# LayerNorm gains and biases in two fused VectorE operations ahead of the transposes, in place of a pass on GpSimd

## Chip, cores and metric

One core of one Trainium2 chip runs the whole program. The metric is the device time in microseconds of an execution; three timed runs of the kernel before are given, and their median is the time that the change is compared with.

## What is computed

Two blocks of a transformer of 512 tokens by 1024 features in float32, four layers in all: latent attention (mla), differential attention (diff), a pooling and gated-convolution mixer (even), and a forgetting attention with a conformer convolution (odd). Behind each mixer comes a SwiGLU feed-forward layer (ffn). Each of the eight steps ends in a sum and a LayerNorm:

```python
h = layernorm(alpha * h + mixer(h), ln_mix_g, ln_mix_b)
h = layernorm(alpha * h + swiglu(h), ln_ffn_g, ln_ffn_b)
# layernorm(x, g, b) = (x - mean(x)) * rsqrt(var(x) + 1e-5) * g + b, over the 1024 features
```

## The kernel before

The residual stream stays in on-chip memory as four tiles `res[t]` of 128 tokens (on partitions) by 1024 features. The products run on TensorE; every float32 operand is given as a high and a low part of 12 significant bits, and each product is three matmuls (`mm3`, L371 to L373). So each weight unit of 512 KB is loaded by the queue of SyncE into `wraw`, copied by ScalarE into the high part `whi` (L170) and subtracted by VectorE or GpSimd into the low part `wlo` (L171). ffn forms its first product by seven products of quarters (Winograd's form), for which VectorE adds and subtracts quarters of the features (`XQ`, L759 to L762, L768) and of the weights (L193 to L198).

Seven of the eight LayerNorms go through `class Norm`, token tile after token tile, within `project_out` (the last one is `LastNorm`, untouched here). For tile t the steps are: the sum with the mixer's product, with row sums (`add_res`, L431); the mean (L448); the squares on ScalarE (L452); the root, a small VectorE operation (L387) and a power on GpSimd (L389, result `lnr`); `scale` (L458), one VectorE operation over 128 x 1024; eight transposes on TensorE into two banks of PSUM (`turn`, L399); `apply` (L464 to L473), which multiplies by the gain and adds the bias of each feature, features being on partitions now, as eight operations over 128 x 128, four on ScalarE (L471) and four on VectorE (L473); then the high parts on ScalarE (L485) and the low parts on VectorE (L489) of the features that the next step's products read (`xh`, `xl`). Ahead of an ffn `apply` also writes the quarters `XQ`, and the high and low parts are taken from them; elsewhere it works in place in PSUM.

`scale` leaves `res[t]` without gain and bias. They come in a separate pass, since only the next sum needs them: `affine_one` (L527 to L532) multiplies and adds over 128 x 512, four operations per tile. Behind the norms of mla, diff, even and odd, `ffn` runs the pass for four tiles on GpSimd, queued at its start behind all that GpSimd has; within odd it runs on GpSimd too, one tile per head; within diff and even it runs on VectorE (`affine`).

```python
def affine_one(eng):
    t, g, b = AFFINE.pop(0)
    for c in range(2):
        s = slice(c * S, (c + 1) * S)
        eng.tensor_mul(res[t][:, s], res[t][:, s], g[:, s])
        eng.tensor_add(res[t][:, s], res[t][:, s], b[:, s])
```

Within `project_out` the order of TensorE, VectorE and ScalarE is the order in which the code is written (`by_hand`); elsewhere the framework's scheduler orders instructions by a timeline of its own, and GpSimd's queue always. Each engine works through its queue in order. The gains and biases of the next norm are loaded into one buffer each (`lng`, `lnb`, L419) by GpSimd's queue, as soon as the pass on the last norm has read them; those of mla by SyncE's. In `project_out`, the first projections of the next step run for tokens 0 to 255 of four weight units, with the transposes of tile 3 behind the second of them, and then for tokens 256 to 511.

Of the kernel before, what the change touches and what calls it, by code (L numbers as in the profile page):

```python
# [50 lines left out]
# the norms in their order  # L51
# [34 lines left out]
# the hidden units of a feed-forward layer in the groups that go into the second product together  # L86
# [3 lines left out]
def ffn_order():  # L90
    """("gate", "up" | "win", unit) of the first product and ("down", columns, pair of chunks) of the second, in turns"""
    order, todo = [], deque()
    for k0, k1 in GROUPS:
        every = (k1 - k0) / len(todo) if todo else 0
        at = every
        for j in range(k0, k1):
            order += [("gate", j), ("up", j)] if j < STD else [("win", j)]
            while todo and j - k0 + 1 >= at - 1e-6:
                order.append(todo.popleft())
                at += every  # L100
        todo.extend(("down", c, u) for c in range(2) for u in range(k0 // 2, k1 // 2))
# [31 lines left out]
class Ring:  # L133
    """A pool's tiles of one tag"""
# [8 lines left out]
class Weights:  # L143
    """Units of weights in the order of their use: each is loaded, and split exactly into two
    parts of 12 significant bits, ahead of its use."""
# [28 lines left out]
    def steps(self):  # L174
        """The next unit, step by step"""
# [10 lines left out]
        # the sums of the quarters, over the quarters that are not needed any more  # L186
# [25 lines left out]
    def may(self, n):  # L212
        """whether one of the next n units is still to be seen to"""
# [100 lines left out]
def kernel(ctx: ExitStack, tc: tile.TileContext, a: dict, out: bass.AP):  # L314
# [15 lines left out]
    def bank(use):  # L330
        """a bank of PSUM, in turns of those for the use"""
# [43 lines left out]
    def split(h, l, src, scale=None):  # L375
        """h + l = src * scale, exactly, in two parts of 12 significant bits."""
# [7 lines left out]
    def rsqrt(ssum, n, count, eps, name):  # L384
        """(ssum / count + eps) ** -0.5 on [P, n]"""
# [6 lines left out]
    def turn(t, bank):  # L392
        """Token tile t of the residual stream with the features on partitions, in two banks"""
# [40 lines left out]
    AFFINE = []  # L434

    class Norm:
        """The LayerNorm of the residual stream, of token tile after token tile, in steps for the
        engines' queues to be laid out by hand"""
        count = 0

        def __init__(self, gb, xT, junk):
            self.gb, self.xT, self.junk, self.ln = gb, xT, junk, Norm.count
            self.m, self.r, self.ps = {}, {}, {}
            Norm.count += 1
# [30 lines left out]
        def source(self, t, c):  # L475
            if XQ:
                return XQ[c, t // 2][:, :, t % 2 * P:(t % 2 + 1) * P]
            return self.ps[t][c].rearrange("p (j t) -> p j t", j=4)

        def parts(self, t, c):  # L480
            return (*part_of(self.xT, t, c), self.source(t, c))
# [8 lines left out]

    class LastNorm:
        """The same behind the last sum, to the output"""
# [28 lines left out]
    def affine():  # L521
        """The gains and biases of the last norm for the residual stream, that only the next sum needs"""
        with after_last():
            while AFFINE:
                affine_one(nc.vector)

    def affine_one(eng):  # L527
        t, g, b = AFFINE.pop(0)
        for c in range(2):
            s = slice(c * S, (c + 1) * S)  # L530
            eng.tensor_mul(res[t][:, s], res[t][:, s], g[:, s])
            eng.tensor_add(res[t][:, s], res[t][:, s], b[:, s])  # L532
# [15 lines left out]
    def mark(*name):  # L548
        """a place in the tensor engine's work, that other work can be queued behind"""
# [8 lines left out]
    class Part:  # L558
        """res = (ALPHA *) res + chunks^T @ w for four chunks, in pieces queued behind marks"""
# [17 lines left out]
    def project_out(chunks, key, gb, xT, names, room, first=True, tail=4, pin=None):  # L577
# [3 lines left out]
        norm = LastNorm(gb, room[0]) if xT is None else Norm(gb, xT, lambda: room[0].tile([P, D], BF16, name="junk", tag=room[1], bufs=room[2]))  # L581
        ps = {}
        cols = {t: ((None, 0, S),) for t in range(NT)}
        if nu == 2:
            # all the weights at hand: one token tile after the other
# [11 lines left out]
            if xT is None:  # L597
# [4 lines left out]
                # the last products are done in two parts  # L602
# [48 lines left out]
        with by_hand():  # L651
            # where the tiles turn: behind two tiles' products, where those of tile 1 are short
            wait = 2 if nu == 2 else 1
            for t in range(NT):
# [3 lines left out]
                if t:  # L658
                    norm.scale(t - 1)
                if t == wait == 2:  # L660
                    norm.turn(0)
                    norm.apply(0, 1)
                    norm.apply(0, 0)
                    norm.high(0, 0)
                    norm.high(0, 1)
                if 1 < t and wait == 1:
                    norm.low(t - 2, 0)
                    norm.low(t - 2, 1)
# [3 lines left out]
                if 1 < t and wait == 2:  # L672
                    norm.low(t - 2, 0)
                    norm.low(t - 2, 1)
# [5 lines left out]
                if t >= wait:  # L680
# [1230 lines left out]
```

## Time and profile before

| what | value |
|---|---|
| timed runs | 2359.85, 2362.2, 2364.51 us; median 2362.2 us |
| profiled execution, first to last instruction (its span) | 2351.2 us |
| TensorE (PE) busy | 2264.4 us, 96% of the span |
| VectorE (DVE) busy | 1842.2 us, 78% |
| ScalarE (ACT) busy | 1033.3 us, 44% |
| GpSimd (POOL) busy | 621.4 us, 26% |
| TensorE's granted clock, mean | 0.985 of 2.4 GHz |

Of the profiled execution the span is given and no other time; the median of the timed runs lies 11.0 us above it. A busy share is a mean over stages: TensorE leads everywhere, so the question in each stage is where it stands still and what it waits for. Matmuls overlap in the records (one that takes 0.28 us starts 0.12 us behind the last), so idle time in a row is slightly less than the start that was lost. Engines are named PE, PEld (weight load), DVE, ACT, POOL and SP in the rows; L12 is line 12 of the kernel before.

### The profile page before, as it was taken

The page shows a single profiled execution, that of the slowest core. Times are in us where ns is not written, and L with a number is a line of the kernel's source. Part 1 is how long each engine was busy: PE and PEld are TensorE (multiplying, and loading weights), DVE is VectorE, ACT ScalarE, POOL GpSimd, SP SyncE. Part 2 cuts the span into 40 slices and gives each one's busy share as a digit, 9 for nine tenths or more (in the row PEclk, how much of TensorE's full clock was granted, in tenths as well). Part 3 has the DMA queues.
Part 4 walks back from the last instruction along what each step waited for, and adds up shares of the span by engine and source line. Part 5 has one row for each costly group of instructions (what it writes and reads, how often), then busy time and mean ns, then how long its engine had stood idle before and what let it go on. Part 6 is the DMA issues. An engine that isn't in the chain of part 4 may idle for free. (4 is left out here: it accounts for less than half of the span.)

```text
span 2351.2 us, 35591 instructions
## 1 busy us (share of the span) xinstructions
PE 2264.4 (96%) x14148; PEld 1996.1 (85%) x14148; DVE 1842.2 (78%) x2810; ACT 1033.3 (44%) x1761; POOL 621.4 (26%) x360
## 2 busy tenths in 40 slices
PE   8999899999999999999999989999997999999997
PEld 8878899998888778999988889999886767899996
DVE  5667888886766688888875698888677767989886
ACT  4654444345555453434353344443344655344441
POOL 2103311112321161111210051111236844311112
PEclk9999999999999999999999999999998999999999
DMA  5212333332321123333323233333222112333331
GB/s 176 61 37 72 99 108 108 98 95 85 99 72 63 37 75 114 108 100 99 98 90 95 92 101 104 108 99 108 81 76 73 36 54 81 108 104 105 99 99 63
DMA packets 59367, 210.52 MB, mean 90 GB/s; under 512 B 6624, under 2 KB 6880, under 8 KB 59200
## 3 DMA queue, kind: packets, MB, share of 16 engines
q1 hardware_dynamic: 56304, 198.97, 26.7%
q0 software_dynamic: 2320, 8.23, 1.0%
q8 instruction: 111, 1.82, 0.3%
q10 hardware_dynamic: 576, 1.05, 0.1%
q14 instruction: 56, 0.46, 0.1%
HBM read 206.12 MB, written 2.10 MB: 89 GB/s over the span
## 5 line engine op out<-in xcount | busy, mean ns | idle before, releaser
L170 ACT ACTIVATE whi<-wraw 128x1024 fp32r<-128x1024 f32 (+3 forms) x528 | 519.8, 987 | 830.8 <-DMA wraw<-in_gu_dram 260.9
L171 POOL TENSOR_TENSOR wlo<-wraw,whi 128x1024 fp32r<-128x1024 f32 (+2 forms) x141 | 358.2, 2544 | 1198.5 <-ACT whi L170 991.1
L171 DVE TENSOR_TENSOR wlo<-wraw,whi 128x1024 fp32r<-128x1024 f32 (+3 forms) x387 | 447.9, 1158 | 140.4 <-ACT whi L170 139.1
L372 PE MATMUL acc<-xl,whi 128*128 128x256 f32 (+1 forms) x1712 | 527.1, 308 | 11.1 <-DVE xl L489 11.1
L373 PE MATMUL acc<-xh,wlo 128*128 128x256 f32 (+1 forms) x1712 | 525.4, 307 | 5.8 <-DVE wlo L171 5.8
L371 PE MATMUL acc<-xh,whi 128*128 128x256 f32 (+1 forms) x1712 | 529.7, 309 | 0.0
L372 PEld LDWEIGHTS acc<-xl,whi 128*128 128x128 f32 x1712 | 325.5, 190 | 37.7 <-DVE xl L489 13.5
L371 PE MATMUL acc<-xs,whi 128*128 128x256 f32 x1216 | 342.6, 282 | 13.7 <-ACT sums L790 7.6
L373 PE MATMUL acc<-xs,wlo 128*128 128x256 f32 x1216 | 344.7, 283 | 3.0 <-DVE wlo L171 3.0
L371 PEld LDWEIGHTS acc<-xh,whi 128*128 128x128 f32 x1712 | 325.5, 190 | 24.2 <-issue 0.4
L373 PEld LDWEIGHTS acc<-xh,wlo 128*128 128x128 f32 x1712 | 325.4, 190 | 23.0 <-DVE wlo L171 6.5
L372 PE MATMUL acc<-xql,whi 128*128 128x256 f32 x1216 | 342.6, 282 | 0.0
L371 PEld LDWEIGHTS acc<-xs,whi 128*128 128x128 f32 x1216 | 231.1, 190 | 21.1 <-ACT sums L790 10.6
L372 PEld LDWEIGHTS acc<-xql,whi 128*128 128x128 f32 x1216 | 229.8, 189 | 5.6
L373 PEld LDWEIGHTS acc<-xs,wlo 128*128 128x128 f32 x1216 | 229.9, 189 | 3.8 <-DVE wlo L171 3.8
L371 PE MATMUL tr<-whi,hh 128*128 128x512 f32 (+1 forms) x296 | 118.6, 401 | 0.0
L372 PE MATMUL tr<-wlo,hh 128*128 128x512 f32 (+1 forms) x296 | 117.4, 397 | 0.0
L373 PE MATMUL ps<-whi,hl 128*128 128x512 f32 x288 | 114.1, 396 | 3.0 <-DVE hl L379 3.0
L373 PE MATMUL tr<-whi,hl 128*128 128x512 f32 (+1 forms) x296 | 116.1, 392 | 0.0
L371 PE MATMUL ps<-whi,hh 128*128 128x512 f32 x288 | 113.4, 394 | 0.3 <-ACT hh L378 0.3
L372 PE MATMUL ps<-wlo,hh 128*128 128x512 f32 x288 | 113.2, 393 | 0.0
L194 DVE TENSOR_TENSOR wraw<-wraw 128x512 f32<-128x512 f32 x76 | 109.2, 1437 | 0.1
(360 smaller groups left out, 4379.9 us busy)
## 6 DMA issues: line engine op xcount, KB each, us to landing
wraw<-in_gu_dram SPq DMA_DIRECT2D x176, 512.0 KB, 3.6
wraw<-in_dn_dram SPq DMA_DIRECT2D x88, 512.0 KB, 3.5
wraw<-in_ev_in_dram SPq DMA_DIRECT2D x16, 512.0 KB, 3.4
wraw<-in_mla_o_dram SPq DMA_DIRECT2D x8, 512.0 KB, 3.6
wraw<-in_df_q_dram SPq DMA_DIRECT2D x8, 512.0 KB, 3.6
wraw<-in_df_k_dram SPq DMA_DIRECT2D x8, 512.0 KB, 3.5
wraw<-in_df_v_dram SPq DMA_DIRECT2D x8, 512.0 KB, 3.4
wraw<-in_df_o_dram SPq DMA_DIRECT2D x8, 512.0 KB, 3.5
```

The costliest lines, as they stand in the source:

```text
L170: self.nc.scalar.activation(hi, raw[:, o:o + n], AF.Copy)
L171: eng.tensor_sub(lo, raw[:, o:o + n], hi.bitcast(F32))
L194: nc.vector.tensor_sub(a21, a11, a21)
L371: nc.tensor.matmul(ps, ah, bh, start=first, stop=False)
L372: nc.tensor.matmul(ps, ah, bl, start=False, stop=False)
L373: nc.tensor.matmul(ps, al, bh, start=False, stop=last)
```

## The change

`scale`, `apply` and the separate pass go. In their place VectorE forms `y = (res - mean) * g` (`gains`), which does not need the root and is queued ahead of it, and, when the root is there, `res = y * r + b` (`biases`), each over 128 x 1024 (in odd as two halves, in buffers that are free there). The tiles that are transposed are then the finished ones; the high and low parts come straight from PSUM, and ahead of an ffn two copies per tile (`keep`) fill the quarters, one on ScalarE and one on VectorE. Cut to its core (comment lines, which go too, and equal edits of the other mixers left out):

```diff
-        def scale(self, t):
-            nc.vector.tensor_scalar(res[t], res[t], self.m[t][:, 2:3], self.r[t], op0=OP.add, op1=OP.mult)
-            AFFINE.append((t, *self.gb))
+        def gains(self, t):
+            self.y = self.room()
+            for s, y in self.y:
+                nc.vector.scalar_tensor_tensor(y, res[t][:, s], self.m[t][:, 2:3], self.gb[0][:, s], op0=OP.add, op1=OP.mult)
+
+        def biases(self, t):
+            for s, y in self.y:
+                nc.vector.scalar_tensor_tensor(res[t][:, s], y, self.r[t], self.gb[1][:, s], op0=OP.mult, op1=OP.add)
...
-        def apply(self, t, c):
-            for j in range(4):
-                o = 16 * self.ln + 4 * c + j
-                p = self.ps[t][c][:, j * P:(j + 1) * P]
-                y = self.source(t, c)[:, j]
-                if c == 0:
-                    nc.scalar.activation(y, p, AF.Identity, scale=par("ln", o), bias=par("ln", o + 8))
-                else:
-                    nc.vector.tensor_scalar(y, p, par("ln", o), par("ln", o + 8), op0=OP.mult, op1=OP.add)
+        def keep(self, t, c):
             if XQ:
-                return XQ[c, t // 2][:, :, t % 2 * P:(t % 2 + 1) * P]
-            return self.ps[t][c].rearrange("p (j t) -> p j t", j=4)
+                y = XQ[c, t // 2][:, :, t % 2 * P:(t % 2 + 1) * P]
+                (nc.vector.tensor_copy if c else nc.scalar.copy)(y, self.parts(t, c)[2])
...
+        def spread(self, t):
+            self.high(t, 0)
+            self.keep(t, 1)
+            self.high(t, 1)
+            self.keep(t, 0)
...
                 if t:
-                    norm.scale(t - 1)
+                    norm.biases(t - 1)
...
                 norm.mean(t)
...
+                norm.gains(t)
                 if t == NT - 1:
                     W.ahead(2)
                 if t >= wait:
                     norm.turn(t - 1)
                 norm.square(t)
-                if t >= wait:
-                    norm.apply(t - 1, 1)
                 norm.root(t)
...
-            with after_last(mybir.EngineType.Pool):
-                while AFFINE:
-                    affine_one(nc.gpsimd)
...
-            affine()
...
-                        if AFFINE and h > 0 and qb == 0:
-                            affine_one(nc.gpsimd)
```

How VectorE's queue moves, at the last tile (`res_81` is tile 3) of mla's norm; L171 is the low part of a weight unit, `lns` the sums and the mean, `lnv` what the root is taken of, `lnr` the root, `lny` the new buffer. Before:

```order
L448 TENSOR_SCALAR lns<-lns 128x1
L489 TENSOR_TENSOR xl<-xq,xh 128x4x128 x2
L171 TENSOR_TENSOR wlo<-wraw,whi 128x1024
L473 TENSOR_SCALAR xq<-tr,sm 128x128 x4
L387 TENSOR_SCALAR lnv<-lns 128x1
L171 TENSOR_TENSOR wlo<-wraw,whi 128x1024
L458 TENSOR_SCALAR res_81<-res_81,lns,lnr 128x1024
L489 TENSOR_TENSOR xl<-xq,xh 128x4x128 x2
L171 TENSOR_TENSOR wlo<-wraw,whi 128x1024
L473 TENSOR_SCALAR xq<-ps,sm 128x128 x4
```

and with the change (L445 is the mean, L481 the low parts, L457 `gains`, L461 `biases`, L470 `keep`):

```order
L445 TENSOR_SCALAR lns<-lns 128x1
L481 TENSOR_TENSOR xl<-ps,xh 128x4x128 x2
L457 SCALAR_TENSOR_TENSOR lny<-res_81,lns,lng 128x1024
L171 TENSOR_TENSOR wlo<-wraw,whi 128x1024
L387 TENSOR_SCALAR lnv<-lns 128x1
L171 TENSOR_TENSOR wlo<-wraw,whi 128x1024
L470 COPY xq<-tr 128x4x128
L461 SCALAR_TENSOR_TENSOR res_81<-lny,lnr,lnb 128x1024
L481 TENSOR_TENSOR xl<-tr,xh 128x4x128 x2
L171 TENSOR_TENSOR wlo<-wraw,whi 128x1024
L470 COPY xq<-ps 128x4x128
L481 TENSOR_TENSOR xl<-ps,xh 128x4x128 x2
```

`gains` stands ahead of the first of the weight units, `biases` where `scale` stood, one copy takes the place of four operations, and the low parts read PSUM (`tr`, `ps`).

GpSimd's queue at the same place; `lnr` is the power of tiles 0 to 3, `res_78` to `res_81` are the four tiles, L171 is the first weight unit that GpSimd splits in ffn. Before:

```order
L389 TENSOR_TENSOR lnr<-lnv,mhalf 128x1 x4
L531 TENSOR_TENSOR res_78<-res_78,lng 128x512 x2
L531 TENSOR_TENSOR res_79<-res_79,lng 128x512 x2
L531 TENSOR_TENSOR res_80<-res_80,lng 128x512 x2
L532 TENSOR_TENSOR res_78<-res_78,lnb 128x512
L531 TENSOR_TENSOR res_81<-res_81,lng 128x512
L532 TENSOR_TENSOR res_78<-res_78,lnb 128x512
L531 TENSOR_TENSOR res_81<-res_81,lng 128x512
L532 TENSOR_TENSOR res_79<-res_79,lnb 128x512 x2
L532 TENSOR_TENSOR res_80<-res_80,lnb 128x512 x2
L532 TENSOR_TENSOR res_81<-res_81,lnb 128x512 x2
L419 DMA lng<-in_ln_ffn_g_dram 128x1024
```

and with the change:

```order
L389 TENSOR_TENSOR lnr<-lnv,mhalf 128x1 x3
L419 DMA lng<-in_ln_ffn_g_dram 128x1024
L389 TENSOR_TENSOR lnr<-lnv,mhalf 128x1
L419 DMA lnb<-in_ln_ffn_b_dram 128x1024
L171 TENSOR_TENSOR wlo<-wraw,whi 128x1024 x23
```

The sixteen operations are gone; the load of the next gains now stands ahead of the last tile's power, and waits for `gains` of tile 3; the load of the biases stands behind it, and waits for `biases`. The same holds at the other norms. In diff's heads, where the scheduler sets the order, some of TensorE's matmuls of neighbouring heads change places too; no matmul is added or taken away.

## Rows read from the trace of the kernel before

**Rows 1.** The page, part 1: engine, busy us (share of the span), instructions.

```profile
PE 2264.4 (96%) x14148; PEld 1996.1 (85%) x14148; DVE 1842.2 (78%) x2810; ACT 1033.3 (44%) x1761; POOL 621.4 (26%) x360
```

**Rows 2.** Stretches: length, busy us by engine; granted clock; DMA share; GB/s.

```profile
209.00:267.00 58.00, 48.78 (x327) 44.30 (x326) 54.64 (x52) 25.80 (x38) 36.27 (x20) 0.97 0.28 92
843.00:901.00 58.00, 50.22 (x327) 45.54 (x326) 54.93 (x53) 26.48 (x38) 36.24 (x20) 0.94 0.27 91
1355.00:1406.00 51.00, 43.86 (x279) 39.83 (x279) 48.44 (x41) 20.43 (x30) 32.49 (x18) 0.93 0.30 93
1976.00:2033.00 57.00, 47.98 (x316) 42.77 (x315) 53.39 (x51) 24.42 (x36) 36.26 (x20) 0.97 0.29 93
```

**Rows 3.** Stretches at other places, same columns.

```profile
575.00:633.00 58.00, 57.77 (x403) 51.56 (x402) 44.93 (x101) 36.90 (x74) 21.31 (x12) 1.00 0.34 108
228.00:231.40 3.40, 3.40 (x17) 3.40 (x18) 3.40 (x2) 0.00 (x0) 3.40 (x3) 0.50 0.00 0
1835.00:1893.00 58.00, 58.00 (x269) 41.72 (x268) 44.34 (x81) 36.64 (x87) 52.66 (x34) 0.91 0.10 30
```

**Rows 4.** Timeline of PE: start, us, instruction [idle before <- releaser].

```profile
210.68 0.39 PE L372 MATMUL acc<-xl,whi 128*128 128x256 f32 x1 [0.64 <-DVE xl L489]
...
217.10 1.09 PE L399 MATMUL ps<-ident,res 128*128 128x128 f32 x8 [0.60 <-DVE res L458]
...
222.71 0.38 PE L373 MATMUL acc<-xh,wlo 128*128 128x256 f32 x1 [1.45 <-DVE wlo L171]
...
227.87 0.50 PE L372 MATMUL acc<-xl,whi 128*128 128x256 f32 x1 [2.18 <-DVE xl L489]
...
255.49 0.50 PE L373 MATMUL ps<-whi,hl 128*128 128x512 f32 x1 [0.79 <-DVE hl L379]
...
258.93 0.39 PE L371 MATMUL acc<-xs,whi 128*128 128x256 f32 x1 [1.52 <-ACT whi L170]
```

**Rows 5.** Timeline of DVE, the same place, same columns.

```profile
211.14 1.22 DVE L171 TENSOR_TENSOR wlo<-wraw,whi 128x1024 fp32r<-128x1024 f32 x1
212.28 1.36 DVE L473 TENSOR_SCALAR xq<-tr,sm 128x128 f32<-128x128 f32 x4
...
215.28 1.77 DVE L458 TENSOR_SCALAR res<-res,lns,lnr 128x1024 f32<-128x1024 f32 x1 [0.44 <-POOL lnr L389]
216.97 3.46 DVE L489 TENSOR_TENSOR xl<-xq,xh 128x512 fp32r<-128x512 f32 x2
220.36 2.30 DVE L171 TENSOR_TENSOR wlo<-wraw,whi 128x1024 fp32r<-128x1024 f32 x1
...
226.06 3.44 DVE L489 TENSOR_TENSOR xl<-xq,xh 128x512 fp32r<-128x512 f32 x2
```

**Rows 6.** Timeline of POOL, the same place, same columns.

```profile
213.85 1.40 POOL L389 TENSOR_TENSOR lnr<-lnv,mhalf 128x1 f32<-128x1 f32 x1 [7.07 <-DVE lnv L387]
215.22 9.84 POOL L531 TENSOR_TENSOR res<-res,lng 128x512 f32<-128x512 f32 x6
...
232.82 13.45 POOL L532 TENSOR_TENSOR res<-res,lnb 128x512 f32<-128x512 f32 x6
246.22 0.77 POOL L419 DMA_DIRECT2D lng<-in_ln_ffn_g_dram  x1
```

**Rows 7.** DVE groups by shape, 300 to 540 us: busy, mean ns | idle.

```profile
L171 DVE TENSOR_TENSOR wlo<-wraw,whi 128x1024 fp32r<-128x1024 f32 x46 | 56.1, 1219 | 14.1 <-ACT whi L170 14.1
```

**Rows 8.** Single lines: count, ns min/median/max, first and last start, forms.

```profile
L458 DVE TENSOR_SCALAR res<-res,lns,lnr x28: 808/812/1769, 196.3 to 1981.7; 128x1024 f32<-128x1024 f32 x28
...
L489 DVE TENSOR_TENSOR xl<-tr,xh x12: 679/681/684, 570.1 to 1719.2; 128x512 fp32r<-128x512 f32 x12
...
L1400 DVE SCALAR_TENSOR_TENSOR cv<-gl,sm,cv x90: 732/743/2802, 1742.0 to 1926.4; 128x512 f32<-128x512 f32 x90
...
L531 POOL TENSOR_TENSOR res<-res,lng x40: 1277/1726/2276, 215.2 to 1997.0; 128x512 f32<-128x512 f32 x40
L531 DVE TENSOR_TENSOR res<-res,lng x16: 677/680/2896, 619.6 to 1309.5; 128x512 f32<-128x512 f32 x16
```

More of the change, by code (lines that the diff above doesn't have):

```diff
@@ L432, in add_res, with __init__ @@
                                        accum_out=SUMS[t][:, c:c + 1] if sums else None)
-    AFFINE = []
     class Norm:
-        count = 0
-        def __init__(self, gb, xT, junk):
-            self.gb, self.xT, self.junk, self.ln = gb, xT, junk, Norm.count
+        def __init__(self, gb, xT, junk, room):
+            self.gb, self.xT, self.junk, self.room = gb, xT, junk, room
             self.m, self.r, self.ps = {}, {}, {}
-            Norm.count += 1
         def mean(self, t):
@@ L489, in low, with lows @@
             nc.vector.tensor_sub(l, p, f32(h))
+        def spread(self, t):
[3 more added lines that the diff above has]
+            self.keep(t, 0)
+        def lows(self, t):
+            self.low(t, 0)
+            self.low(t, 1)
     class LastNorm:
@@ L519, in out @@
                 q.dma_start(out[0, t * P:(t + 1) * P, s], y)
-    def affine():
-        with after_last():
-            while AFFINE:
[L525 to L532, printed above, removed]
     def some(ps, t, chunks, k0, k1, w, o=0, n=S):
@@ L575, in emit, with whole, project_out @@
                 add_res(ps, t, c, True, False)
-    def project_out(chunks, key, gb, xT, names, room, first=True, tail=4, pin=None):
+    def whole(p, tag, bufs):
+        return lambda: [(slice(0, D), p.tile([P, D], F32, name="lny", tag=tag, bufs=bufs))]
+    def project_out(chunks, key, gb, xT, names, room, between=None, first=True, tail=4, pin=None):
         nu = len(chunks) // 2
-        norm = LastNorm(gb, room[0]) if xT is None else Norm(gb, xT, lambda: room[0].tile([P, D], BF16, name="junk", tag=room[1], bufs=room[2]))
+        norm = LastNorm(gb, room[0]) if xT is None else Norm(gb, xT, lambda: room[0].tile([P, D], BF16, name="junk", tag=room[1], bufs=room[2]), between)
         ps = {}
@@ L658, in project_out @@
                 if t:
-                    norm.scale(t - 1)
+                    norm.biases(t - 1)
                 if t == wait == 2:
                     norm.turn(0)
[L662 to L665, printed above, removed]
+                    norm.spread(0)
                 if 1 < t and wait == 1:
-                    norm.low(t - 2, 0)
-                    norm.low(t - 2, 1)
+                    norm.lows(t - 2)
                 products(t, 1)
@@ L672, in project_out @@
                 if 1 < t and wait == 2:
-                    norm.low(t - 2, 0)
-                    norm.low(t - 2, 1)
+                    norm.lows(t - 2)
+                norm.gains(t)
                 if t == NT - 1:
@@ L685, in project_out @@
                 if t >= wait:
-                    norm.apply(t - 1, 0)
-                    norm.high(t - 1, 0)
-                    norm.high(t - 1, 1)
+                    norm.spread(t - 1)
             t = NT - 1
-            norm.scale(t)
-            norm.low(t - 1, 0)
-            norm.low(t - 1, 1)
+            norm.biases(t)
+            norm.lows(t - 1)
             W.ahead(4)
@@ L700, in project_out @@
                     norm.turn(t)
-                    norm.apply(t, 0)
-                    norm.high(t, 0)
-                    norm.apply(t, 1)
-                    norm.high(t, 1)
-                    norm.low(t, 0)
-                    norm.low(t, 1)
+                    norm.spread(t)
+                    norm.lows(t)
                     W.ahead(5)
@@ L751, in ffn @@
                 finish(j, ps[2 * j], ps[2 * j + 1])
-            with after_last(mybir.EngineType.Pool):
-                while AFFINE:
-                    affine_one(nc.gpsimd)
             gb = ln_params("ln_ffn" + ("_2" if key == "2" else ""), i)
@@ L853, in ffn @@
             last = [chunks[k] for k in range(*GROUPS[-1])]
-            return nxt, project_out(last, "down", gb, nxt, names, (fp, "sums", 2), first=False)
+            return nxt, project_out(last, "down", gb, nxt, names, (fp, "sums", 2), whole(fp, "sums", 2), first=False)
     def mla(xT, close_x, open_x, names):
@@ L1052, in mla @@
             with pool("mla_n") as np_:
-                return nxt, project_out([O[h] for h in range(4, 8)], "mla_o", gb, nxt, names, (np_, "junk", 1), first=False,
+                return nxt, project_out([O[h] for h in range(4, 8)], "mla_o", gb, nxt, names, (np_, "junk", 1), whole(np_, "lny", 1), first=False,
                                         pin=pin("mla", OPIN["mla"]))
@@ L1277, in diff @@
             with pool("df_n") as np_:
-                return nxt, project_out([O[h] for h in range(4, 8)], "df_o", gb, nxt, names, (np_, "junk", 2), first=False,
+                return nxt, project_out([O[h] for h in range(4, 8)], "df_o", gb, nxt, names, (np_, "junk", 2), whole(np_, "lny", 1), first=False,
                                         pin=pin("df", OPIN["df"]))
@@ L1345, in even @@
                 A[j] = h, l
-            affine()
             nxt = open_x()
-            return nxt, project_out([A[j] for j in range(4)] + [B[j] for j in range(4)], "ev_o", gb, nxt, names, (ep, "y", 2))
+            return nxt, project_out([A[j] for j in range(4)] + [B[j] for j in range(4)], "ev_o", gb, nxt, names, (ep, "y", 2), whole(ep, "lny", 1))
     def odd(xT, open_x, FIRST, names):
@@ L1756, in odd @@
             C = D_
+            between = [(slice(c * S, (c + 1) * S), cv[c]) for c in range(2)]
             region.close()
@@ L1759, in odd @@
             nxt = open_x()
-            return nxt, project_out(C, "od_o", gb, nxt, names, (op_, "e3", 1), first=False)
+            return nxt, project_out(C, "od_o", gb, nxt, names, (op_, "e3", 1), lambda: between, first=False)
     xs = ExitStack()
```

3 lines of the change are left out of this document (1 added, 2 removed).

## The prediction

> **What bounds the kernel now.** I read the page's busy shares first: TensorE is at work for 2264.4 of 2351.2 us [rows 1]. So it leads, and a change pays only where TensorE stands still or runs at a lower clock. I then cut the span into stretches and looked for both. In the 58 us around the handover from the first ffn to diff TensorE is idle for 58.00 - 57.77 = 0.2 us, at clock 1.00 [rows 3]. The four handovers from a mixer to its ffn, by contrast, have 58 - 48.78 = 9.2, 58 - 50.22 = 7.8, 51 - 43.86 = 7.1 and 57 - 47.98 = 9.0 us of idle time, 33.2 us together, with a clock of 0.97, 0.94, 0.93 and 0.97 [rows 2]. The clock loses (1 - 0.97) x 58 = 1.7, then 3.5, 3.6 and 1.7 us, 10.5 us together. So 43.7 us lie in these four places. The reader should also see VectorE there: 54.64 of 58 us busy.
>
> Next I asked TensorE's timeline at the first of them what it waits for. In order, it waits 0.64 us for a low part of the features, 0.60 for `scale`, 1.45 for a low part of weights, 2.18 for the low parts of tile 3, and later 0.79 for a low part of the hidden units and 1.52 for ScalarE's high part of weights [rows 4]. All but the last are VectorE. Right behind the wait of 2.18 us, from 228.0 to 231.4 us, the granted clock is 0.50, the lower of its two levels [rows 3].
>
> VectorE's timeline says why. At 211.14 us a weight split takes 1.22 us; at 220.36 the same form takes 2.30. Two low parts take 3.46 us at 216.97, `scale` 1.77 [rows 5]; elsewhere a low part takes 0.68 and `scale` 0.81 [rows 8], and in the middle of the ffn 46 weight splits average 1.219 us [rows 7]. What differs is GpSimd: the pass of gains and biases begins at 215.22 us and ends where the load of the next gains is issued, at 246.22 [rows 6]. Over these 31 us VectorE's operations with two inputs in on-chip memory take nearly twice their time. GpSimd's own operations stretch too, from 1.28 to a median of 1.73 us [rows 8].
>
> **What goes, comes and moves.** Per tile, VectorE loses `scale` (0.81) and the four operations of `apply` (1.36 together) [rows 5, 8]. It gains `gains` and `biases`. No row shows this form over 128 x 1024. The nearest: a subtraction of that size with two inputs takes 1.22 [rows 7]; the fused form over 128 x 512 takes at least 0.73 against 0.68 of a two-input operation [rows 8]; so I take 1.22 + 0.05 = 1.27, with 0.81 (the one-input `scale`) and 2.30 (a disturbed split) as ends. Ahead of an ffn it also gains one copy from PSUM, for which I take the 0.68 of a low part from PSUM [rows 8]; the ends are 0.34 (one of the four it replaces) and 1.36 (all four). So 16 tiles ahead of an ffn change by 2 x 1.27 + 0.68 - 2.17 = +1.05 us, 16.8 together; 12 other tiles by +0.37, 4.4 together; and 32 operations of the pass that were VectorE's own, in diff and even, go at 0.68 each, -21.8. VectorE's work is the same within a microsecond. Only its place matters. ScalarE gets four operations less and one copy more per tile; it is no leader, so I price that at nothing.
>
> Now the last tile of mla's norm, with VectorE's new order and undisturbed times, from 211.14 us on: `gains` 1.27, split 1.15, root 0.1, split 1.15, copy 0.68 bring `biases` to 215.5, and it ends at 216.8. `scale` ended at 217.05, so TensorE's wait for it shrinks from 0.60 to 0.35: **0.25 us** gained, little, for the two fused operations cost nearly what the pass's disturbance did there. Two low parts then end at 218.1 and the split at 219.3. TensorE wanted that split at 222.71 - 1.45 = 221.3: **1.45 us** gained. The copy ends at 220.0 and the low parts of tile 3 at 221.3; TensorE wanted them at 227.87 - 2.18 = 225.7, less the 1.7 gained so far: 224.0. **2.18 us** gained, with 2.7 to spare, and with these waits the fall of the clock, **1.7**. Behind that VectorE is some 8 us ahead of its old place (it ended the same low parts at 229.5), so the waits of 0.79 and 1.52 go too: what makes the weight's high part late is a chain of VectorE's additions.
>
> Over the four handovers: 43.7, less what stays. The first wait, 0.64 in three of the four (in even the low parts come earlier), depends on the last sum and not on the pass: 1.9. Of the 9.2 us at the first handover the waits listed above make 7.2; of the other 2.0, which hang on ScalarE and on loads, I let half stay, 4.0 in all. And I allow 0.5 each for new waits, 2.0. That leaves **35.8 us**. In odd's heads the pass is sixteen operations of up to 1.73 us, about half of GpSimd's 52.66 us in a stretch where the clock, at 0.91, loses 5.2 us [rows 3]: I take half, rounded to **3**, between 0 and 5.2. In diff and even VectorE loses 21.8 us of work at places where TensorE seldom waits: **1**, between 0 and 2. The norms behind an ffn gain and lose nothing while two units' projections cover them: there `biases` is 0.46 longer than `scale`; uncovered, over all 28 tiles, that would be 12.9 us.
>
> The Trainium skill, "VectorE: DVE Perf Modes", section "The perf-mode tier table", speaks against the change: over 2048 float32 elements a one-source operation takes 1227 ns and a two-source one 2293. An estimate by that ratio makes each fused operation 0.81 x 1.87 = 1.5 us, and the sum some 2 us smaller; the rows give 1.22, so the sum goes by these.
>
> GpSimd's queue: the load of the next gains now stands ahead of the last power. `gains` of tile 3 ends at 212.4, the issue takes 0.77, the power at most 1.40 [rows 6], ending by 214.6, 0.9 ahead of need: nothing. The load of the biases behind it holds back only a weight split that TensorE wants much later. The loads take a share of bandwidth from weights; the 2.7 us above cover it.
>
> The sum is 35.8 + 3 + 1 = 40 us: 2311 us of span, and with the 11.0 us that lie between it and the median, **2322 us** against 2362.2.
>
> **The rivals.**
>
> *Half of it.* The later waits come from loads and ScalarE, not from VectorE's delay. For it: the 1.52 us is a wait for ScalarE [rows 4]. Against: its inputs come through VectorE. Then a handover gains 0.25 + 1.45 + 2.18 + 1.7 = 5.6, 22.4 in all, and with 4 more elsewhere and 2 of new waits, -24: 2338 us.
>
> *Issue in the way.* The load of the next gains delays the last power, at all seven norms. It has 0.77 + 0.9 = 1.7 us before the transposes of tile 3 wait. GpSimd's disturbed operations reach 2.28 [rows 8]; an issue that long costs 0.6 each, 4 in all: 2326. For it: it stands in that queue now; against: the row of 0.77 fell among VectorE's two-input operations. The Trainium skill, "SBUF — State Buffer", section "SBUF: two separate sides", has such a mechanism: a load issued by GpSimd starves while VectorE runs a one-source operation in its fast mode. By that rule it would not strike here, as no such long operation is left in the place; no run shows it yet.
>
> *Slower.* The doubling is not the pass's doing but belongs to the place (weights and features moving at once), and stays at 2.30. Then the last tile's path grows by 2.30 for `gains`, 2.30 - 1.77 for `biases` and 0.68 - 1.36 for the copy: 2.15 us at four handovers, 8.6, and 1.1 at the three others, 2372 us. It decides once two-input operations stay above about 1.9 us. Against it: the same split at 1.22 just ahead of the pass, at the same place [rows 5].
>
> *Nothing.* VectorE is earlier, but the ffn's rate is set by loads and the time is given back: 2358 to 2362. Against: TensorE's idle time in the handover is not made up later by anything that waits.
>
> **How the numbers follow.** The forecast has 0.55, half of it 0.24, the issue 0.07, nothing 0.06, slower 0.08. A measurement of this kernel can tell about 0.2% (4.7 us) from no change; so faster 0.86, same 0.06, slower 0.08. The range runs from 2308, where all 43.7 us, odd's 5.2, diff's and even's 2 and some start time that idle rows do not count go (-54), to 2342, the half gain with its 4 us elsewhere left out; it holds some 8 in 10.
>
> **What would show it.** Right: in the handovers splits of 128 x 1024 at 1.2 us and low parts at 0.7 throughout, no operation over `lng` on GpSimd, the wait for tile 3's low parts gone, the clock at 1.00, idle time of 2 to 3 us each. `gains` and `biases` near 1.27, the copy near 0.68. Wrong: fused operations of 1.5 us or more, a wait for `biases` of over 0.6, or a load of weights that ends a wait where `scale` did.

## The result, and the profile after

The changed kernel takes 2304.84 us, median of four runs (2299.79 to 2305.86), beside 2362.15 of the kernel before on the same chip (four runs, 2359.85 to 2364.51). The medians lie 57.3 us apart; the ratio on record is 0.9772 with an interval of 0.9751 to 0.9792, which is 54 us less (49 to 59). On a later occasion it was 0.9767 (0.9741 to 0.9794), with 2300.76 beside 2358.26. The forecast was 2322 us in 2308 to 2342: the sign was right, 40 us were forecast, and the median lies 3.2 us below the range. The profiled execution has a span of 2302.4 us and a time of 2304.18.

The page of the changed kernel, busy time by engine; [rows 1] is the same line of before:

```profile
PE 2250.3 (98%) x14148; PEld 1988.6 (86%) x14148; DVE 1770.4 (77%) x2718; ACT 997.1 (43%) x1665; POOL 471.3 (20%) x280
```

VectorE is 71.8 us less busy although it took over what GpSimd did: it has 92 operations fewer, by the forecast's sum about the same work, and what remains is quicker. GpSimd lost 150 us.

TensorE's matmuls come in nearly the same order and in the same number, so the stages can be cut at the same work: from the first transposition of one norm to that of the next. The stretches of four stages (first ffn, diff, odd and last ffn), columns as in [rows 2], first of the kernel before:

```profile
198.70:563.90 365.20, 353.63 (x2398) 324.43 (x2396) 310.85 (x375) 149.84 (x204) 94.33 (x45) 1.00 0.30 96
563.90:832.10 268.20, 262.81 (x1458) 214.33 (x1457) 183.24 (x468) 149.67 (x370) 60.97 (x40) 0.99 0.23 73
...
1701.60:1965.00 263.40, 244.32 (x1286) 194.96 (x1285) 183.03 (x345) 136.34 (x280) 145.32 (x91) 0.94 0.21 65
1965.00:2351.20 386.20, 362.76 (x2445) 331.48 (x2444) 328.81 (x409) 146.65 (x200) 97.51 (x49) 0.98 0.29 92
```

Then of the changed kernel:

```profile
198.20:551.10 352.90, 350.62 (x2398) 322.67 (x2396) 298.49 (x367) 146.18 (x192) 63.10 (x29) 1.00 0.33 102
551.10:817.90 266.80, 260.95 (x1456) 212.59 (x1456) 170.63 (x440) 143.00 (x354) 58.27 (x40) 0.99 0.23 69
...
1664.10:1927.90 263.80, 247.37 (x1284) 198.69 (x1285) 181.93 (x334) 129.45 (x264) 123.00 (x75) 0.93 0.20 61
1927.90:2302.40 374.50, 359.68 (x2445) 329.96 (x2444) 317.13 (x407) 142.65 (x188) 67.45 (x33) 0.99 0.31 98
```

All stage lengths in us, cut in this way, of these two and of the experiments below (each stage runs from its mixer's or ffn's input norm; the last ends with the span):

| kernel | mla | ffn 1 | diff | ffn 2 | even | ffn 3 | odd | ffn 4 | span |
|---|---|---|---|---|---|---|---|---|---|
| before | 194.6 | 365.2 | 268.2 | 364.1 | 140.2 | 365.2 | 263.4 | 386.2 | 2351.2 |
| before, again (e1) | 193.6 | 367.0 | 266.7 | 364.2 | 140.7 | 365.2 | 268.0 | 386.8 | 2356.3 |
| changed | 194.0 | 352.9 | 266.8 | 352.4 | 140.7 | 353.1 | 263.8 | 374.5 | 2302.4 |
| changed, again (e10) | 195.0 | 353.0 | 266.4 | 353.2 | 141.0 | 353.0 | 258.6 | 374.5 | 2299.0 |
| changed + two-input pass (e2) | 195.4 | 363.4 | 265.3 | 363.2 | 140.8 | 364.5 | 258.4 | 385.3 | 2340.4 |
| changed + one-input pass (e3) | 193.9 | 356.4 | 264.9 | 356.9 | 141.1 | 356.5 | 258.7 | 377.2 | 2310.0 |
| before, thin pass (e4) | 196.1 | 351.8 | 263.8 | 350.8 | 140.1 | 352.0 | 267.9 | 372.1 | 2298.4 |
| before, pass on VectorE (e5) | 193.4 | 358.8 | 265.3 | 358.7 | 139.2 | 361.8 | 267.0 | 380.7 | 2328.9 |
| changed, two-input pass later (e8) | 194.4 | 360.2 | 266.5 | 358.5 | 140.9 | 360.8 | 264.7 | 380.7 | 2330.9 |

The four ffns lose 12.3, 11.7, 12.1 and 11.7 us, 47.8 of the 48.8 by which the spans differ. No mixer moves by more than 1.4.

The handovers themselves, from the same point behind the first transposition and over the same lengths as in [rows 2], in the changed kernel:

```profile
208.40:266.40 58.00, 56.41 (x404) 52.54 (x403) 50.30 (x62) 29.77 (x39) 5.96 (x5) 1.00 0.39 128
828.80:886.80 58.00, 57.13 (x408) 53.18 (x408) 50.94 (x63) 30.07 (x40) 6.38 (x5) 1.00 0.37 127
1329.60:1380.60 51.00, 50.69 (x359) 47.22 (x359) 45.44 (x52) 25.44 (x34) 5.64 (x3) 1.00 0.38 126
1938.90:1995.90 57.00, 55.55 (x392) 51.17 (x391) 50.07 (x64) 28.20 (x38) 4.96 (x4) 1.00 0.38 130
```

TensorE idles 1.6, 0.9, 0.3 and 1.5 us in them, 4.2 together where it was 33.2, at clock 1.00.

TensorE at the first handover (timeline, as [rows 4]) waits for this and no more:

```profile
210.10 0.39 PE L372 MATMUL acc<-xl,whi 128*128 128x256 f32 x1 [0.64 <-DVE xl L481]
216.11 1.06 PE L399 MATMUL ps<-ident,res 128*128 128x128 f32 x8 [0.18 <-DVE res L461]
221.04 0.38 PE L373 MATMUL acc<-xh,wlo 128*128 128x256 f32 x1 [0.76 <-DVE wlo L171]
```

VectorE there (timeline, as [rows 5]):

```profile
210.56 1.28 DVE L457 SCALAR_TENSOR_TENSOR lny<-res,lns,lng 128x1024 f32<-128x1024 f32 x1
211.75 1.22 DVE L171 TENSOR_TENSOR wlo<-wraw,whi 128x1024 fp32r<-128x1024 f32 x1
...
214.08 0.69 DVE L470 COPY xq<-tr 128x512 f32<-128x512 f32 x1
214.68 1.28 DVE L461 SCALAR_TENSOR_TENSOR res<-lny,lnr,lnb 128x1024 f32<-128x1024 f32 x1
215.91 1.29 DVE L481 TENSOR_TENSOR xl<-tr,xh 128x512 fp32r<-128x512 f32 x2
219.76 1.23 DVE L171 TENSOR_TENSOR wlo<-wraw,whi 128x1024 fp32r<-128x1024 f32 x1 [2.56 <-ACT whi L170]
```

The split that took 2.30 us in [rows 5] takes 1.23, and VectorE has time to wait for ScalarE ahead of it. ScalarE's timeline shows that it waits in turn for the load of that weight unit:

```profile
218.66 1.06 ACT L170 ACTIVATE whi<-wraw 128x1024 fp32r<-128x1024 f32 x1 [2.78 <-DMA wraw<-in_gu_dram]
```

GpSimd's queue there (timeline, as [rows 6]):

```profile
212.15 0.77 POOL L419 DMA_DIRECT2D lng<-in_ln_ffn_g_dram  x1 [5.80 <-DVE lny L457]
213.19 1.40 POOL L389 TENSOR_TENSOR lnr<-lnv,mhalf 128x1 f32<-128x1 f32 x1 [0.28 <-DVE lnv L387]
216.27 0.58 POOL L419 DMA_DIRECT2D lnb<-in_ln_ffn_b_dram  x1 [1.68 <-DVE res L461]
```

The issue of the gains' load is over at 212.92, and the power behind it still waits 0.28 us for VectorE: the load is not in its way.

### The profile page after: what moved, and what is told of

Its sections match the earlier page's. It is cut to its first block, busy times and chain, and to the rows that moved or that the text cites. A ratio compares the mean times of both kernels' runs of the same rounds, so it can differ in the third digit from the quotient of the medians.

```text
span 2302.4 us, 35345 instructions
## 1 busy us (share of the span) xinstructions
PE 2250.3 (98%) x14148; PEld 1988.6 (86%) x14148; DVE 1770.4 (77%) x2718; ACT 997.1 (43%) x1665; POOL 471.3 (20%) x280
## 5 line engine op out<-in xcount | busy, mean ns | idle before, releaser
L171 POOL TENSOR_TENSOR wlo<-wraw,whi 128x1024 fp32r<-128x1024 f32 (+2 forms) x141 | 355.8, 2526 | 1281.4 <-ACT whi L170 1030.2
L171 DVE TENSOR_TENSOR wlo<-wraw,whi 128x1024 fp32r<-128x1024 f32 (+3 forms) x387 | 429.3, 1110 | 136.8 <-ACT whi L170 136.1
L431 DVE SCALAR_TENSOR_TENSOR res<-res,acc 128x512 f32<-128x512 f32 x87 | 58.9, 683 | 55.2 <-PE acc L373 54.9
```

The lines of the kernel that those rows point to most:

```text
L171: eng.tensor_sub(lo, raw[:, o:o + n], hi.bitcast(F32))
L431: nc.vector.scalar_tensor_tensor(y, y, ALPHA if first else 1.0, ps, op0=OP.mult, op1=OP.add, accum_out=SUMS[t][:, c:c + 1] if sums else None)
```

## The experiments

**e1. The kernel before, profiled again.** No edit.

> The kernel before, unchanged, profiled once more. Its profiled span was 2351.2 us while its timed runs had a median of 2362.2; the changed kernel's profiled span is 2302.4 and its median 2304.8. If the profiled execution of before was merely a quick one, this span comes out near 2360 and the spans then differ by some 57 us like the times; then some stage other than the four handovers must be longer in it. If profiling itself makes before quicker, the span is near 2351 again.

Measured: span 2356.3 us, time 2358.03, and thirteen timed runs of before on this chip from 2351.41 to 2364.13 (median 2354.86). Against the first profile the odd mixer is 4.6 us longer and the first ffn 1.8; the handovers cost the same. So executions of one program differ by some 13 us, and the first profile was a quick one: its span lies 11.0 us under the median, of which e1 shows 1.7 to lie outside the span. The profiled execution of e1 is 3.2 us over the median of its chip, so profiling does not make this kernel quicker.

**e2. The contention put back.** In the changed kernel; `OLD` keeps the last norm's gains and biases, which nothing reads any more. The order of the other engines stays; the loads of the next gains and biases wait for the additions.

```diff
+        OLD[0] = g, b
...
+            with after_last(mybir.EngineType.Pool):
+                g, b = OLD[0]
+                for k in range(16):
+                    s = slice(k % 2 * S, (k % 2 + 1) * S)
+                    nc.gpsimd.tensor_add(g[:, s], g[:, s], b[:, s])
             gb = ln_params("ln_ffn" + ("_2" if key == "2" else ""), i)
```

> The changed kernel, with sixteen additions of 128x512 with two inputs put on GpSimd at each of the four mixer-to-ffn handovers, where the pass of before stood (they add the old biases to the old gains, which nothing reads any more; the loads of the next gains and biases then wait for them as in before). Theory (the pass slowed VectorE's operations with two inputs): weight splits of 128x1024 go from 1.22 to about 2.3 us for some 30 us, each ffn grows by 9 to 12 us again, total 2341 to 2353 us. Rival (what counted was VectorE's new order and the operations that apply() no longer issues, not GpSimd): the splits stay at 1.22 and the total at 2303 to 2310.

Measured: 2345.53 us (ratio to before 0.9958, 0.9939 to 0.9977). The ffns grow by 10.5, 10.8, 11.4 and 10.8 us, 43.5 of the 47.8 that the change had taken off. GpSimd's timeline at the first handover:

```profile
215.89 31.35 POOL L740 TENSOR_TENSOR lng<-lng,lnb 128x512 f32<-128x512 f32 x16
```

VectorE's timeline over the same 31 us:

```profile
226.40 2.31 DVE L171 TENSOR_TENSOR wlo<-wraw,whi 128x1024 fp32r<-128x1024 f32 x1
228.64 2.32 DVE L746 TENSOR_TENSOR xq<-xq 128x1024 f32<-128x1024 f32 x1
...
237.59 0.68 DVE L720 TENSOR_TENSOR sums<-sums,acc 128x512 f32<-128x512 f32 x1
238.19 1.73 DVE L754 TENSOR_TENSOR xql<-xq,xs 128x1024 fp32r<-128x1024 f32 x1
...
246.01 1.78 DVE L171 TENSOR_TENSOR wlo<-wraw,whi 128x512 fp32r<-128x512 f32 x1
```

Nothing else had changed, and the splits are at 2.31 us again. The size of the addition is telling: 2.31 - 1.22 = 1.09 over 1024 columns, 1.78 - 0.69 = 1.09 over 512. It is an amount per instruction, not a factor. The addition that reads its second input from PSUM (`acc`) keeps its 0.68, and the operation right behind it waits less, 1.73 - 1.22 = 0.51.

**e3. The same with one input.** The edit is against e2.

```diff
-                    nc.gpsimd.tensor_add(g[:, s], g[:, s], b[:, s])
+                    nc.gpsimd.tensor_scalar(g[:, s], g[:, s], 1.0, None, op0=OP.mult)
```

> As the kernel with sixteen two-input additions on GpSimd at each handover, but with sixteen operations that read one tensor of 128x512, times 1.0, in place. If any read by GpSimd disturbs VectorE's operations with two inputs, the splits stretch here too, by as long as these operations run: 2325 to 2353 us. If it takes two inputs on both engines, splits stay at 1.22 and the total within 2303 to 2312 us. I lean to the first, 0.6.

Measured: 2316.89 us (0.9841, 0.9823 to 0.986). The ffns grow by 3.5, 4.5, 3.4 and 2.7 us, 14.1 together. VectorE's timeline:

```profile
223.45 1.62 DVE L171 TENSOR_TENSOR wlo<-wraw,whi 128x1024 fp32r<-128x1024 f32 x1
...
238.87 1.09 DVE L171 TENSOR_TENSOR wlo<-wraw,whi 128x512 fp32r<-128x512 f32 x1
```

Again an amount per instruction, 1.62 - 1.22 = 1.09 - 0.69 = 0.40 us. So a one-input operation on GpSimd disturbs too, by less than half; I had not separated the two prices, and the total falls between the ranges of the two theories.

**e4. The kernel before with hardly any pass.** It leaves the gains and biases out of all but 4 of each 512 columns of the residual stream, on VectorE in diff and even too.

```diff
             s = slice(c * S, (c + 1) * S)
+            s = slice(c * S, c * S + 4)
             eng.tensor_mul(res[t][:, s], res[t][:, s], g[:, s])
             eng.tensor_add(res[t][:, s], res[t][:, s], b[:, s])
```

> The kernel before, with the separate pass over only 4 of each 512 columns (so the residual stream lacks gains and biases elsewhere): all waits and the order remain, the work on GpSimd and VectorE goes. Theory: each of the four ffns takes some 353 us instead of 365 as in the changed kernel, and the total is 2310 to 2318 us, within 10 of the changed kernel's 2304.8. Rival (the gain came from the fused operations ahead of the transposes): at least half of the 57 us stays, 2333 us or more. The stage of the odd mixer should stay at 263 to 264 us although its sixteen operations on GpSimd are gone, if its clock has other reasons; my forecast had put 3 us on them, which would make it 260 to 261.

Measured: 2292.42 us (0.9744, 0.9725 to 0.9764). The ffns take 351.8, 350.8, 352.0 and 372.1 us: 13.4, 13.3, 13.2 and 14.1 less than before, without any fused operation. So the gain is the pass's going. The total lies 18 us under the 2310 that I had expected at the least: the ffns fell further than the 353 us that I had taken for them, and the rest of the difference was not traced. The changed kernel, which does compute the gains and biases, gives 1.1 to 2.4 us of it back per ffn. The odd mixer takes 267.9 us with a thin pass:

```profile
1658.40:1926.30 267.90, 249.99 (x1285) 199.01 (x1285) 182.98 (x345) 136.44 (x280) 125.01 (x91) 0.92 0.21 64
```

Its clock, 0.92, is no better than with the pass (0.94 and, in e1, 0.92).

**e5. The pass on VectorE, not fused.**

```diff
-            with after_last(mybir.EngineType.Pool):
-                while AFFINE:
-                    affine_one(nc.gpsimd)
-            gb = ln_params("ln_ffn" + ("_2" if key == "2" else ""), i)
...
                 X[k] = hi, lo
+            affine()
+            gb = ln_params("ln_ffn" + ("_2" if key == "2" else ""), i)
```

> The kernel before, whose separate pass at the four mixer-to-ffn handovers goes to VectorE, sixteen operations at about 0.68 us = 10.9 us of VectorE's time, queued behind the low parts of the feature sums instead of on GpSimd (in the odd mixer it stays where it was). Theory (the gain is that GpSimd no longer works beside VectorE, whatever form the affine part has): the four ffns take 351 to 357 us each instead of 364 to 386 with the last, total 40 to 52 us below the kernel before. Rival (the fused operations are needed, because 10.9 us more on VectorE at that place bring waits of their own): half of it or less, under 25 us.

Measured: 2329.22 us (0.9883, 0.9854 to 0.9912), 27.7 us less than before: neither end. The ffns win 6.4, 5.4, 3.4 and 5.5 us. VectorE's timeline shows the pass at its plain price:

```profile
239.04 4.89 DVE L531 TENSOR_TENSOR res<-res,lng 128x512 f32<-128x512 f32 x8
...
245.06 4.90 DVE L532 TENSOR_TENSOR res<-res,lnb 128x512 f32<-128x512 f32 x8
```

Against e4 those 9.8 us cost 7.0 to 9.8 us in each of the first three ffns and 8.6 in the last: VectorE's time behind a handover is TensorE's time. So the form seems to matter after all, for what it costs VectorE; the place of that work differs too, and no run parts the two.

**e6. All weight splits off GpSimd.** In the changed kernel.

```diff
-            on_pool = (name in ONPOOL) != (self.at - 1 in OTHERWISE)
+            on_pool = False
```

> The changed kernel with all of GpSimd's 141 weight splits (2526 ns each, 355.8 us) on VectorE, where one of this size takes 1.22 us: 141 x 1.15 = some 160 us more for VectorE, less what the two-input operations beside them no longer lose (in the ffns one neighbour stretches from 1.22 to 2.90 or from 0.69 to 2.84 us for each split on GpSimd, +1.7 to +2.2). If that holds for most of them, VectorE's busy time falls or stays within 40 us of 1770 and the total is 2290 to 2305. Rival: the splits stand in VectorE's queue behind waits that they did not have on GpSimd, and in the mixers the total grows: 2305 to 2330. I lean to the rival for the mixers, 0.6, and to no change in the ffns.

Measured: 2302.07 us (0.9771, 0.9748 to 0.9795), the changed kernel's time within scatter. The first line of its page:

```profile
PE 2248.1 (98%) x14148; PEld 1986.6 (86%) x14148; DVE 1752.8 (76%) x2859; ACT 995.4 (43%) x1665; POOL 116.6 (5%) x139
```

VectorE does 141 operations more and is 17.6 us less busy. GpSimd's splits had cost it more than they spared it, but the time hung on neither.

**e7. The norms behind an ffn as before, the others changed.**

```diff
         def biases(self, t):
+            if self.room is None:
+                nc.vector.tensor_scalar(res[t], res[t], self.m[t][:, 2:3], self.r[t], op0=OP.add, op1=OP.mult)
+                AFFINE.append((t, *self.gb))
+                return
...
-            return nxt, project_out(last, "down", gb, nxt, names, (fp, "sums", 2), whole(fp, "sums", 2), first=False)
+            return nxt, project_out(last, "down", gb, nxt, names, (fp, "sums", 2), None, first=False)
```

With it come the old `apply`, a `gains` that does nothing for these norms, and the calls of `affine()` and `affine_one()` in diff, even and odd.

> The changed kernel, but the three norms behind an ffn in the form of the kernel before (scale, apply, and the separate pass in the mixer behind: on VectorE in diff and even, on GpSimd, one tile per head, in odd). In the changed kernel TensorE waits there 0.49 + 0.55 + 0.89 + 0.88 = 2.8 us in the first place and 2.7 in the two others, in the kernel before 1.0 in each. Theory (uncovered, the fused pair costs more on the path than scale alone): 3 x 1.75 = 5 us less, 2297 to 2302 us against 2304.8. Rival: the pass in diff and even, 10.9 us of VectorE each, takes as much back: 2303 to 2308.

Measured: 2308.23 us (0.9784, 0.9752 to 0.9816; runs from 2297.01 to 2310.0): no gain. What it was to remove was there. TensorE's timeline of the changed kernel at the end of the first ffn:

```profile
551.06 1.09 PE L399 MATMUL tr<-ident,res 128*128 128x128 f32 x8 [0.32 <-DVE res L461]
555.34 1.09 PE L399 MATMUL ps<-ident,res 128*128 128x128 f32 x8 [0.40 <-DVE res L461]
563.67 0.39 PE L372 MATMUL acc<-xl,whi 128*128 128x256 f32 x1 [0.64 <-DVE xl L481]
574.49 0.39 PE L373 MATMUL acc<-xh,wlo 128*128 128x256 f32 x1 [0.71 <-DVE wlo L171]
```

And that of e7 at the same place:

```profile
564.79 1.07 PE L399 MATMUL tr<-ident,res 128*128 128x128 f32 x8 [0.41 <-DVE res L480]
566.15 0.39 PE L372 MATMUL acc<-xl,whi 128*128 128x256 f32 x1 [0.17 <-DVE xl L504]
```

The waits shrank by 1.5 us here, from 2.07 to 0.58, and by as much at the two other norms. But, cut like the stages above, diff took 267.0 us in place of 266.8 and even 138.7 in place of 140.7, and the odd mixer took 269.1 in place of 263.8, which is more than all of that.

**e8. The contention in the middle of the ffn.** The same sixteen operations of e2's kind (added and subtracted again), at hidden unit 10.

```diff
             for j in range(NFF):
...
+                if j == 10:
+                    with after_last(mybir.EngineType.Pool):
+                        for n in range(16):
+                            s = slice(n % 2 * S, (n % 2 + 1) * S)
+                            (nc.gpsimd.tensor_add if n // 2 % 2 == 0 else nc.gpsimd.tensor_sub)(gb[0][:, s], gb[0][:, s], gb[1][:, s])
```

> The changed kernel with the same sixteen two-input operations of 128x512 on GpSimd in each ffn, but in its middle, at its tenth hidden unit, some 100 us behind the handover (they add the biases to the gains and subtract them again; the orders of TensorE, VectorE and ScalarE are unchanged). At the handover such operations cost 43.5 us over four ffns. VectorE's two-input operations must double here as well. If it costs time wherever VectorE is busy (it is busy 87% of the 58 us that followed the handover, so some 30 us of it at double price leave a backlog of 10 us or more), each ffn takes 358 to 364 us in place of 353: total 2325 to 2350. If the weights split ahead cover it away from the handover, the ffns stay within 2 us and the total at 2303 to 2312.

Measured: 2331.69 us (0.9874, 0.9844 to 0.9905). The ffns grow by 7.3, 6.1, 7.7 and 6.2 us, 27.3 in all, against 43.5 at the handover. So the disturbance costs in the middle of the ffn too, nearly two thirds of what it costs at the handover. That weights split ahead cover the rest there was not shown. TensorE's timeline shows the late sums:

```profile
360.53 0.39 PE L371 MATMUL acc<-xs,whi 128*128 128x256 f32 x1 [0.86 <-ACT sums L768]
368.84 0.39 PE L371 MATMUL acc<-xh,whi 128*128 128x256 f32 x1 [1.23 <-DVE sums L771]
```

**e9, e10, e11. A version with fewer splits on GpSimd, beside the changed kernel.**

```diff
+            on_pool = on_pool and name not in ("down", "gate", "up") and not name.startswith("od_")
```

> The changed kernel with GpSimd's weight splits put on VectorE in the ffns and the odd mixer alone; in mla and diff they stay on GpSimd, since with all of them moved mla took 196.2 us (194.0 in the changed kernel) and diff 268.3 (266.9). Expected: mla and diff as in the changed kernel, ffns 352 to 353, total 2298 to 2303 us; no difference that can be told from the changed kernel's 2304.8 if mla's and diff's 2 us were scatter.

> The changed kernel, unchanged, timed beside the version with fewer splits on GpSimd on one chip. Each ffn again at 352 to 354 us but the last (374 to 375), the odd mixer anywhere between 257 and 269 us by its clock, the median 2300 to 2306 us.

> The changed kernel with the ffns' and the odd mixer's splits of GpSimd on VectorE, once more, beside the changed kernel. If the 4.9 us by which its median lay under that of the changed kernel (2299.98 against 2304.84, on different occasions) are its own, 3 to 6 us less than the changed kernel now; if they were scatter of the odd mixer's clock, within 2 us.

Measured: e9 2299.98 us (0.9744, 0.9719 to 0.9768); then side by side e10, the changed kernel, 2300.76 (0.9767, 0.9741 to 0.9794) and e11, e9's kernel, 2302.93 (0.9773, 0.975 to 0.9796). The 4.9 us of e9 were scatter, and no version that computes the same beats the changed kernel measurably.

## Why the prediction was right, and where it was short

**The cause** was the right one. e2 gives back 43.5 of 47.8 us by adding nothing but two-input work on GpSimd (and the wait of the next loads for it), e4 takes 13 to 14 us per ffn by thinning nothing but that work there. The slower rival (the doubling belongs to the place) is out: e2 and the changed kernel have the same place. The rule that fits in the main is in the Trainium skill, "SBUF — State Buffer", section "Who interferes with whom": a VectorE instruction with two inputs in SBUF and a GpSimd instruction that reads SBUF exclude each other for a whole instruction, and one with at most one such input outside the fast modes goes free. Beside two-input work the rows agree: where both queues are full, each such VectorE instruction waits a fixed 1.09 us, nearly the 1.28 us of the quickest operation of the pass on GpSimd [rows 8]; low parts and sums that read PSUM stay at 0.68, and in e2 operations of 1024 columns follow each other every 2.24 us (226.40, 228.64). `scale`, with one input, went from 0.81 to 1.77 in [rows 5, 8]; the same section counts the fast mode of such an operation among those that collide. Beside one-input work the pairs that collide are the same, but not for a whole instruction: no such operation of e3 took GpSimd under 1.48 us, and VectorE waited 0.40. I had read the rows as "nearly twice", which is a factor; an amount per instruction is what they show.

**The prices** of the new operations: `gains` and `biases` were put at 1.27 and the copy at 0.68. Measured (single lines, columns as in [rows 8]):

```profile
L457 DVE SCALAR_TENSOR_TENSOR lny<-res,lns,lng x24: 1275/1284/1289, 193.7 to 1677.9; 128x1024 f32<-128x1024 f32 x24
...
L461 DVE SCALAR_TENSOR_TENSOR res<-lny,lnr,lnb x24: 1276/1284/3082, 195.7 to 1680.8; 128x1024 f32<-128x1024 f32 x24
...
L470 DVE COPY xq<-tr x8: 681/684/687, 201.3 to 1945.4; 128x512 f32<-128x512 f32 x8
```

The estimate by the ratio in the Trainium skill, "VectorE: DVE Perf Modes", section "The perf-mode tier table" (1.5 us, 2 us off the sum), was too dear: the row of a two-input operation of the same size was the better guide.

**The last tile** went as worked out but for one wait: TensorE's wait for the finished rows of `res` was to fall from 0.60 to 0.35 and fell to 0.18, that of 2.18 us is gone and the clock is at 1.00. The wait of 1.45 for a split was to go and 0.76 of it stays; its releaser is VectorE, but VectorE waits 2.56 us for ScalarE's high part there, and ScalarE 2.78 us for the load. So at this one wait the rival that loads come in behind VectorE was right, for half of the 1.45 us.

**The handovers, 35.8 us forecast, 47.8 measured.** This is the step that failed, and by size alone. The budget of 43.7 us was read from four stretches that ended at 267, 901, 1406 and 2033 us. In these four, cut at the same work, 4.2 us of idle time stayed where I had let 7.9 stay. And the same pile-up goes on behind them. The next stretches of before, columns as in [rows 2]:

```profile
267.00:325.00 58.00, 55.65 (x398) 51.78 (x397) 50.71 (x63) 24.30 (x32) 9.14 (x4) 1.00 0.32 100
901.00:955.00 54.00, 52.81 (x379) 49.23 (x378) 47.53 (x58) 21.67 (x29) 8.27 (x3) 1.00 0.32 108
1406.00:1460.00 54.00, 52.73 (x379) 49.14 (x379) 47.97 (x59) 22.25 (x30) 8.27 (x3) 1.00 0.35 108
2033.00:2090.00 57.00, 55.52 (x398) 51.66 (x397) 50.11 (x62) 23.73 (x31) 8.27 (x3) 1.00 0.32 102
```

TensorE idles 2.35, 1.19, 1.27 and 1.48 us in them, 6.3 together. By the stage rows (length less busy PE) the first ffn's idle time fell from 11.6 to 2.3 us and the last one's from 23.4 to 14.8; over the four it is 33 us less, and TensorE's busy time 15 less. Of these 15, some 10.5 are the clock, as forecast, since the four handovers now run at 1.00; the rest I take to be start time that idle rows do not count, which the text had named and had put into the range alone. No run measures that rest by itself.

**The odd mixer, 3 us forecast, not settled.** "I take half" of a clock loss had no row behind it. With a pass (263.4, 268.0), without (263.8, 258.6) and with a thin one (267.9) the stage follows its clock: 263.4 x (1 - 0.94) = 15.8 us lost before, 21.4, 18.5, 12.9 and 21.4 in the others, which leaves 245 to 248 in all five. The thin pass gave nothing back, so the pass's work on GpSimd does not show as the cause of that clock. But over all thirteen traces, cut in the same way, the odd mixer takes 263.4 to 269.1 us (median 267.9) in the five with the old norm ahead of it (before, e1, e4, e5, e7), and 257.7 to 265.3 (median 258.7) in the eight with the new one. The four that the table leaves out are e7 with 269.1, e6 with 257.8, and e9 and e11, one program, with 257.7 and 265.3. The two groups overlap, but a gain of several us is likelier than none, and it would fit what the ratio's 54 us have over the ffns' 47.8. What in the change would raise the clock there is open.

**Diff and even, 1 us forecast:** -1.4 and +0.5 in the profile, so nothing speaks against it, but it is within scatter. **The norms behind an ffn, nothing forecast:** wrong in size. In the 47 us around each of the three TensorE now idles 2.2, 2.1 and 2.0 us, where it was 0.6, 0.7 and 0.6, so the units' projections do not quite cover the new pair; e7, with the old form, is back at 0.6 at each and gains nothing that can be measured. **The issue of loads, nothing forecast:** right, by the timeline of GpSimd at the first handover.

**The 11.0 us between span and median** were carried over as they stood. They were 1.7 us outside the span and, as far as e1 tells, some 9 of a quick execution. The changed kernel's profile has 2.4 there. So of the 17.2 us by which 2322 missed 2304.84, 8.8 are the sum (48.8 against 40) and, up to rounding, 8.6 are this.

## What to carry to other kernels

Work moved to GpSimd is not free because GpSimd is idle: where it reads on-chip memory beside VectorE's two-input operations, each pair can cost VectorE a fixed time per instruction (here up to 1.09 us beside two-input work over 128 x 512, the same for 512 and 1024 columns), so it should be priced as VectorE's own work and put where VectorE has slack. How the moved work is formed and placed on VectorE counts: plain operations kept half of the gain, the fused pair kept nearly all. When a delay is to be priced, follow the waits until the engine that leads has none left, and take several profiles of the kernel before if one of its stages has a clock that scatters.

## What was not expected

Two executions of one program differ mostly in one stage. The stretch of the odd mixer in e1, the kernel before again, columns as above:

```profile
1701.50:1969.50 268.00, 249.37 (x1285) 199.25 (x1285) 184.22 (x345) 136.88 (x280) 146.29 (x91) 0.92 0.20 64
```

And in e10, the changed kernel again:

```profile
1665.90:1924.50 258.60, 240.89 (x1285) 194.02 (x1285) 181.84 (x334) 129.30 (x264) 122.45 (x75) 0.95 0.20 63
```

So it is 263.4 us at a clock of 0.94 and 268.0 at 0.92 in the kernel before, 263.8 at 0.93 and 258.6 at 0.95 in the changed one. What sets these clocks was not tried; it limits what a timing of this kernel can tell to a few microseconds. And that VectorE gets less busy when it takes over 141 operations of GpSimd (e6) was not foreseen.
